# Gate and up projections of the gated layers as 2x2 block products with seven multiplications, down projection in five chunks between them

## The chip, the cores and the metric

The kernel runs on one core of one Trainium2 chip. The metric is device time in microseconds (us), the median of three runs. One execution was profiled; its trace gives the rows below.

## The reference, cut to what matters

Batch 1, 512 tokens, 1024 features, all in float32. A first block (projections, mLSTM, gated MLP, a feed-forward of 4096) is followed by a second block of two layers. Each layer has a gated feed-forward, three attentions and a second gated feed-forward, so there are four gated feed-forwards:

```python
D_FF = 2816

def swiglu(h, w_gate, w_up, w_down):
    return (jax.nn.silu(h @ w_gate) * (h @ w_up)) @ w_down

# in each of the two layers, twice: x = x + 0.5 * swiglu(rmsnorm_2(x, gain), w_gate, w_up, w_down)
```

`rmsnorm_2` scales each token by one number (the reciprocal root of its mean square) and each feature by a gain.

## The kernel before, in words

Activations lie feature-major: a tile is 128 features by 512 tokens, so x is 8 tiles, and the 2816 hidden features are 22 tiles. Every float32 operand of a product is split in a high and a low part (`split`, L201 to L203: ScalarE copies the high part, VectorE subtracts it to get the low one), and each product is three matmuls (`mm3`, L225 to L229: high by high, high by low, low by high). The weights are the stationary operand, 128x128 for one matmul; the activations move, 512 columns at a time. Weights come in units of 128x1024 by DMA on SP's queue (`load_weights`, L209, three raw buffers), and a unit is split in one pass (`split_weights`, L214, three high and three low buffers of 1024).

A gated feed-forward is `ffn` (L870). For each of 22 hidden tiles it takes the gate unit and then the up unit through `gemm_fm` (8 feature tiles by three matmuls of 512 columns each, so 48 matmuls for the pair), into two of three PSUM banks named "g". The operands are `xs`: x times the norm's gain, split, written by the stage ahead of the layer. They lack the norm's factor for each token, `rb`, which is ready only some time into the layer (`norm`, L857, a chain of small steps: sums over features on TensorE, a root on GpSimd, a broadcast on TensorE). So VectorE multiplies both results by `rb` on the way out of PSUM (L885, L887), ScalarE takes the silu, VectorE multiplies the two and the product is split into `hid` (L888, L203). When all 22 tiles are there, the down projection takes each of 8 output tiles through all 22 hidden tiles (66 matmuls in one accumulation, weight units of 8, 8 and 6 tiles), and `residual` (L846) adds half of it to x, writes the next stage's split operands and the square sums. In the last layer the last output tile is done in two halves of 256 tokens, and `g_end` (L918) ends each half: residual, square sums, the final norm, output.

TensorE takes its instructions in the order written, for the first two hidden tiles of a layer (`in_order`, L193). For all else a planner orders the instructions of each engine ahead of time, when the kernel is built. A `Chain` (L104) emits small dependent steps between the products, after a given number of products. The engines then execute their queues in that fixed order. In the first layer the generator behind the norm also multiplies x by the first block's final gain and a second factor `rbx` (L838, eight instructions), and later computes position tables (L950 on).

The lines of `ffn` that the prediction's steps touch:

```python
            self.gemm_fm(og, self.weights(a["w2g"][which, i, 0], KT, P), xs)
            self.gemm_fm(ou, self.weights(a["w2g"][which, i, 1], KT, P), xs)
            while norm.rb is None:
                norm.step()
            ...
            nc.vector.tensor_tensor(t, og, rb, op=ALU.mult)
            nc.scalar.activation(t, t, AF.Silu)
            nc.vector.tensor_tensor(u, ou, rb, op=ALU.mult)
            nc.vector.tensor_tensor(t, t, u, op=ALU.mult)
            self.split(hid[i][0], hid[i][1], t)
```

Of the kernel before, what the change touches and what calls it, by code (L numbers as in the profile page):

```python
# [10 lines left out]
F32 = mybir.dt.float32  # L11
# [20 lines left out]
# columns of the parameter pack  # L32
# [20 lines left out]
# feature-major tiles of the first block's input projection after the first slab  # L53
# [17 lines left out]
# what comes when: the order of the heads and of the projections beside them, the shares of work between two stages of a  # L71
# tile, the products between the steps of a chain, the engines of some elementwise work
# [56 lines left out]
def drain(gen):  # L129
    """run a generator to its end"""  # L130
    while True:
        try:
            next(gen)
        except StopIteration as e:
            return e.value


class Net:
    def __init__(self, ctx, tc, a):
# [11 lines left out]
        self.t, self.chains = 0.0, []  # L151
# [57 lines left out]
    def load_weights(self, src, f):  # L209
        raw = self.wp.tile([P, 1024], F32, name="wraw", tag="wraw", bufs=WBUFS[2])  # L210
        self.last_load = self.nc.sync.dma_start(out=raw[:, :f], in_=src[:, :f])
        return raw

    def split_weights(self, raw, nk, n, pool=False):  # L214
        f = nk * n
        lo = self.wp.tile([P, 1024], F32R, name="wlo", tag="wlo", bufs=WBUFS[0])
        hi = self.wp.tile([P, 1024], F32R, name="whi", tag="whi", bufs=WBUFS[1])
        self.split(hi[:, :f], lo[:, :f], raw[:, :f], pool)
        return (hi[:, :f].rearrange("p (k n) -> p k n", k=nk), lo[:, :f].rearrange("p (k n) -> p k n", k=nk))
# [5 lines left out]
    def mm3(self, out, ah, al, bh, bl, start, stop):  # L225
        mm = self.nc.tensor.matmul
# [1428 lines left out]
```

## Time and profile before

| | |
|---|---|
| median of three runs | 3022.72 us (3022.42 to 3023.36) |
| profiled execution, first to last instruction | 3020.9 us |
| TensorE busy | 2935.9 us, 97%, 13845 matmuls |
| VectorE busy | 1601.3 us, 53% |
| ScalarE busy | 1272.8 us, 42% |
| the four gated layers start at | 873.27, 1571.71, 1942.2 and 2636.4 us |

The profiled execution has no time of its own beside its span; the runs' median is 1.8 us longer than the span. A matmul's duration in the trace holds its way through the array, and the next one starts long before it ends, so the pace of a stream is read from the starts. VectorE's instructions overlap a little in the same way.

### The profile page before, as it was taken

To read this page: it belongs to the slowest core of one execution; us is meant where nothing else is said; L and a number is where in the kernel's file an instruction comes from. 1 tells how busy PE (TensorE), PEld (TensorE's weight loads), DVE (VectorE), ACT (ScalarE), POOL (GpSimd) and SP (SyncE) were. 2 spreads that over 40 slices of the span, in tenths; PEclk is the share of its full clock that TensorE was granted. 3 is DMA by queue.
4 is the path that set the end of the run, shared out by engine and by line. 5 is a ranking of instruction groups with operands and counts; after the bars stand their busy time and mean duration, and the time that the engine had idled before them with its cause. 6 is when DMAs were issued, how large, how long until landed. Compare 5 with 4: busy or idle time off the path is not lost.

```text
span 3020.9 us, 35009 instructions
## 1 busy us (share of the span) xinstructions
PE 2935.9 (97%) x13845; PEld 2387.9 (79%) x13845; DVE 1601.3 (53%) x2388; ACT 1272.8 (42%) x1917; POOL 417.8 (14%) x255
## 2 busy tenths in 40 slices
PE   6999999999999999989999999999999889999998
PEld 5888978888878888876788888888888767888887
DVE  7765665524455443488764443344433887644433
ACT  5665454423333222376743322223223767532322
POOL 4233430000000000243400000000002434100000
PEclk9999999999999999999999999999999999999999
DMA  6334332222223223211022223232322110122222
GB/s 233 111 123 140 137 135 82 92 97 94 95 92 100 92 94 96 89 56 43 29 70 93 96 89 96 94 98 91 96 89 94 57 49 29 63 91 98 92 95 73
DMA packets 79544, 278.06 MB, mean 92 GB/s; under 512 B 8811, under 2 KB 11115, under 8 KB 79380
## 3 DMA queue, kind: packets, MB, share of 16 engines
q1 hardware_dynamic: 79380, 275.82, 28.0%
q8 instruction: 109, 1.79, 0.2%
q14 instruction: 55, 0.45, 0.0%
HBM read 273.69 MB, written 2.10 MB: 91 GB/s over the span
## 4 chain that ended last, share of the span: by engine, by line
PE 89%; DVE 6%; issue 2%; ACT 1%; POOL 1%; DMA 0%; SPq 0%; POOLq 0%; DVEq 0%; ACTq 0%
PE up L227 5%; PE up L229 5%; PE up L228 5%; PE down L228 5%; PE gate L227 5%; PE down L229 5%; PE down L227 5%; PE gate L228 5%; PE gate L229 5%; PE ff L227 4%; PE ff L229 4%; PE ff L228 4%; PE pv L1320 2%; PE ptr L1302 2%; PE wo L229 1%
## 5 line engine op out<-in xcount | busy, mean ns | idle before, releaser
L202 ACT ACTIVATE whi<-wraw 128x1024 fp32r<-128x1024 f32 (+2 forms) x472 | 490.3, 1039 | 1286.9 <-issue 503.1
L203 DVE TENSOR_TENSOR wlo<-wraw,whi 128x1024 fp32r<-128x1024 f32 (+1 forms) x406 | 502.9, 1239 | 428.3 <-ACT whi L202 426.0
L203 POOL TENSOR_TENSOR wlo<-wraw,whi 128x1024 fp32r<-128x1024 f32 (+1 forms) x66 | 155.6, 2361 | 914.8 <-ACT whi L202 903.9
L228 PE MATMUL down<-hid,whi 128*128 128x512 f32 (+1 forms) x726 | 281.6, 388 | 0.0
L229 PE MATMUL down<-hid,wlo 128*128 128x512 f32 (+1 forms) x726 | 281.5, 388 | 0.0
L227 PE MATMUL down<-hid,whi 128*128 128x512 f32 (+1 forms) x726 | 280.9, 387 | 0.0
L887 DVE TENSOR_TENSOR u<-up,rb 128x512 f32<-128x512 f32 x88 | 60.8, 691 | 282.0 <-PE up L229 281.9
L227 PE MATMUL up<-xs,whi 128*128 128x512 f32 x528 | 209.4, 397 | 0.0
L227 PE MATMUL gate<-xs,whi 128*128 128x512 f32 x528 | 208.9, 396 | 0.0
L228 PE MATMUL up<-xs,whi 128*128 128x512 f32 x528 | 208.6, 395 | 0.0
L228 PE MATMUL gate<-xs,whi 128*128 128x512 f32 x528 | 208.5, 395 | 0.0
L229 PE MATMUL up<-xs,wlo 128*128 128x512 f32 x528 | 208.5, 395 | 0.0
L229 PE MATMUL gate<-xs,wlo 128*128 128x512 f32 x528 | 207.8, 394 | 0.0
L272 POOL TENSOR_TENSOR y<-ms,mhalf 128x4 f32<-128x4 f32 (+2 forms) x24 | 27.1, 1128 | 1293.2 <-DVE ms L271 1290.2
L885 DVE TENSOR_TENSOR t<-gate,rb 128x512 f32<-128x512 f32 x88 | 60.8, 691 | 197.5 <-PE gate L229 189.3
L228 PEld LDWEIGHTS down<-hid,whi 128*128 128x128 f32 x726 | 136.4, 188 | 30.7
L227 PEld LDWEIGHTS down<-hid,whi 128*128 128x128 f32 x726 | 136.3, 188 | 30.7
L229 PEld LDWEIGHTS down<-hid,wlo 128*128 128x128 f32 x726 | 136.5, 188 | 29.4
L227 PEld LDWEIGHTS up<-xs,whi 128*128 128x128 f32 x528 | 99.2, 188 | 24.2
L229 PEld LDWEIGHTS up<-xs,wlo 128*128 128x128 f32 x528 | 99.3, 188 | 23.8
L229 PEld LDWEIGHTS gate<-xs,wlo 128*128 128x128 f32 x528 | 99.2, 188 | 23.8
L227 PEld LDWEIGHTS gate<-xs,whi 128*128 128x128 f32 x528 | 99.2, 188 | 23.6
(562 smaller groups left out, 6844.0 us busy)
## 6 DMA issues: line engine op xcount, KB each, us to landing
wraw<-in_w2g SPq DMA_DIRECT2D x176, 512.0 KB, 3.5
wraw<-in_w2d SPq DMA_DIRECT2D x64, 512.0 KB, 3.5
ada<-in_ada SPq DMA_DIRECT2D x48, 512.0 KB, 5.3
wraw<-in_w1f SPq DMA_DIRECT2D x44, 512.0 KB, 3.5
wraw<-in_w1a SPq DMA_DIRECT2D x32, 512.0 KB, 3.4
wraw<-in_w1b SPq DMA_DIRECT2D x32, 512.0 KB, 3.4
wraw<-in_w2f SPq DMA_DIRECT2D x28, 512.0 KB, 3.5
wraw<-in_w2d SPq DMA_DIRECT2D x32, 384.0 KB, 3.0
```

Source lines behind the costliest of these rows:

```text
L202: self.nc.scalar.activation(hi, src, AF.Copy)
L203: (self.nc.gpsimd if pool else self.nc.vector).tensor_tensor(lo, src, hi.bitcast(F32), op=ALU.subtract)
L227: mm(out, ah, bh, start=start, stop=False)
L228: mm(out, ah, bl, start=False, stop=False)
L229: mm(out, al, bh, start=False, stop=stop)
L272: nc.gpsimd.tensor_tensor(y, ms, self.mhalf[:, :n], op=ALU.pow)
L885: nc.vector.tensor_tensor(t, og, rb, op=ALU.mult)
L887: nc.vector.tensor_tensor(u, ou, rb, op=ALU.mult)
L1302: nc.tensor.transpose(tr[:, b * P:(b + 1) * P], p[:, b * P:(b + 1) * P], self.c("ident"))
L1320: nc.tensor.matmul(o, values[b][:, h * P:(h + 1) * P], pt[i][:, b], start=b + i == 0, stop=b + i == NT)
```

## The change

Of the 22 hidden tiles of a gated layer the first three (`PLAIN`) are done as before. For the other 19 the gate and the up tile together are one 2x2 block product: rows gate and up, features 0 to 511 and 512 to 1023, tokens 0 to 255 and 256 to 511. It is computed with 7 products of 4 feature tiles by 256 tokens (84 matmuls of 256 columns) in place of 8 (which would be 48 of 512). The sums of weight blocks are formed for each hidden tile (`g_block_weights`), those of the activations once for each layer (`sums_of`), from x with gain and `rb` in them; all sums are on VectorE. Partial results that several outputs share stay in PSUM while more is added, and are copied out between the products. The last of the seven products of a block is held back until the next block's second product or a down product's third feature tile. The down projection comes in five chunks of hidden tiles, its products standing between the blocks of the next chunk; x is added to after each chunk. Weights for one item are prepared between the products of the item ahead. The high and low parts of a weight unit share one buffer; there are four raw buffers, and 24 big slots in place of 28. In the last layer the last two output tiles of the last chunk end together in two halves of the tokens. TensorE's order is the written one throughout the layer; the other engines stay with the planner.

```diff
-WBUFS = (3, 3, 3)
-SLOTS = 28
+WBUFS = (4, 2, 5, 3)
+SLOTS = 24
+
+CHUNKS = (5, 5, 4, 4, 4)
+
+PLAIN = 3
+H = T // 2
...
     def load_weights(self, src, f):
-        raw = self.wp.tile([P, 1024], F32, name="wraw", tag="wraw", bufs=WBUFS[2])
-        self.last_load = self.nc.sync.dma_start(out=raw[:, :f], in_=src[:, :f])
+        raw = self.wp.tile([P, 1024], F32, name="wraw", tag="wraw", bufs=WBUFS[0])
+        with self.tc.issue_after(self.last_load.ins) if self.last_load else ExitStack():
+            self.last_load = self.nc.sync.dma_start(out=raw[:, :f], in_=src[:, :f])
         return raw
...
+    def kilo(self, name, n):
+        return self.wp.tile([P, 1024 * n], F32R, name=name, tag=f"w{n}k", bufs=WBUFS[1 + n])
...
+    def sums_of(self, up, down, half, pool):
+        v = nc.gpsimd if pool else nc.vector
+        th, tl, b = self.slot("th")[:, :1024], self.slot("tl")[:, :1024], self.slot("bs")[:, :1024]
+        u1, u2, d1, d2 = up[:, :H], up[:, H:], down[:, :H], down[:, H:]
+        ta, tb = self.tmp("ta"), self.tmp("tb")
+        t1, t3, t2, t4 = ta[:, :H], ta[:, H:], tb[:, :H], tb[:, H:]
+        nc.scalar.activation(b[:, :H], u1, AF.Copy)
+        v.tensor_tensor(t1, u2, u1, op=ALU.subtract)
+        v.tensor_tensor(t3, d2, u2, op=ALU.add)
+        nc.scalar.activation(b[:, H:3 * H], down, AF.Copy)
+        v.tensor_tensor(t2, d2, t1, op=ALU.add)
+        v.tensor_tensor(t4, d1, t2, op=ALU.subtract)
+        nc.vector.tensor_tensor(b[:, 3 * H:], u1, b[:, :H].bitcast(F32), op=ALU.subtract)
+        nc.vector.tensor_tensor(half, down, b[:, H:3 * H].bitcast(F32), op=ALU.subtract)
+        for i, t in enumerate((ta, tb)):
+            self.split(th[:, i * T:(i + 1) * T], tl[:, i * T:(i + 1) * T], t, pool)
...
+    def g_block_weights(self, raw):
+        (a21, a22), (a11, a12) = ((r[:, :T], r[:, T:]) for r in raw)
+        s32, s14 = (self.wp.tile([P, 1024], F32, name=name, tag="ws", bufs=WBUFS[1]) for name in ("s32", "s14"))
+        s3, s2, s1, s4 = s32[:, :T], s32[:, T:], s14[:, :T], s14[:, T:]
+        w = {}
+        def part(names, src):
+            n = len(names)
+            t = self.kilo(names[0], n)
+            hi, lo = t[:, :n * T], t[:, n * T:]
+            self.split(hi, lo, src)
...
+        part(["a11"], a11)
+        yield
+        nc.vector.tensor_tensor(s3, a21, a11, op=ALU.subtract)
+        nc.vector.tensor_tensor(s1, a21, a22, op=ALU.subtract)
+        nc.vector.tensor_tensor(s2, a11, s1, op=ALU.subtract)
+        yield
+        part(["s3", "s2"], s32)
+        yield
+        nc.vector.tensor_tensor(s4, a12, s2, op=ALU.subtract)
+        part(["a12"], a12)
+        yield
+        part(["a22"], a22)
+        yield
+        part(["s1", "s4"], s14)
+        yield
...
+    def block(self, w, acts, on, between):
+        def product(out, a, b, first):
+            wh, wl = w[a]
+            n = len(acts)
+            for k in range(n):
+                xh, xl = acts[k][b]
+                self.mm3(out, wh[:, k], wl[:, k], xh, xl, first and k == 0, k == n - 1, skip_group_check=True)
+                self.spend(3 * H * CYCLE)
+            between()
+        e = self.bank("g", "e")[:, :H]
+        product(e, "a11", "b11", True)
+        on("e1", e)
+        g = self.bank("s", "g")[:, :H]
+        product(g, "s3", "t3", True)
+        on("g1", g)
+        self.close_block()
+        product(e, "s2", "t2", False)
+        on("e2", e)
+        f = self.bank("v", "f")[:, :H]
+        product(f, "a12", "b21", True)
+        on("f", f)
+        product(g, "a22", "t4", False)
+        on("g2", g)
+        product(e, "s1", "t1", False)
+        on("e3", e)
+        def last():
+            product(e, "s4", "b22", False)
+            on("e4", e)
...
+        def operands():
+            while norm.rb is None or which == 0 and norm.rbx is None:
+                yield 0.3
+            gains = norm.gain if which == 0 else self.par(("ffn1n0", "ffn2n0", "ffn1n1", "ffn2n1")[which], 0, KT)
+            half = self.halves("xhalf", 4)
+            for k in range(4):
+                t = [self.tmp("xr"), self.tmp("xr")]
+                for i in range(2):
+                    kk = k + 4 * i
+                    nc.vector.scalar_tensor_tensor(t[i], x[:, kk], gains[:, kk:kk + 1], norm.rb, op0=ALU.mult, op1=ALU.mult)
+                    if which == 0:
+                        nc.vector.scalar_tensor_tensor(x[:, kk], x[:, kk], self.par("final1", kk), norm.rbx, op0=ALU.mult, op1=ALU.mult)
+                acts.append(self.sums_of(*t, next(half), False))
+                yield 0.5
+        operands = Chain(self, operands())
...
+        class Up:
...
+            def run(me, w, between):
+                operands.finish()
+                t, u = self.tmp("t"), self.tmp("u")
+                def on(what, o):
+                    if what == "e1":
+                        nc.scalar.activation(t[:, :H], o, AF.Copy)
+                    elif what == "g1":
+                        nc.scalar.activation(u[:, H:], o, AF.Copy)
+                    elif what == "e2":
+                        nc.scalar.activation(u[:, :H], o, AF.Copy)
+                    elif what == "f":
+                        nc.vector.tensor_tensor(t[:, :H], o, t[:, :H], op=ALU.add)
+                        nc.scalar.activation(t[:, :H], t[:, :H], AF.Silu)
+                    elif what == "g2":
+                        nc.vector.tensor_tensor(u[:, :H], o, u[:, :H], op=ALU.add)
+                    elif what == "e3":
+                        nc.vector.tensor_tensor(u[:, H:], o, u[:, H:], op=ALU.add)
+                    else:
+                        nc.scalar.activation(t[:, H:], o, AF.Silu)
+                        nc.vector.tensor_tensor(t, t, u, op=ALU.mult)
+                        keep(me.i, t)
+                self.block(w, acts, on, between)
...
+        class Down:
...
+            def run(me, w, between):
+                o, n = self.bank("g", "down"), me.n
+                act = [hid[me.k0 + k] for k in range(me.nk)]
+                for k, _ in enumerate(self.g_gemm(o, w, act)):
+                    if k == 1:
+                        self.close_block()
+                    between()
+                nc.vector.scalar_tensor_tensor(x[:, n], o, 0.5, x[:, n], op0=ALU.mult, op1=ALU.add)
...
+        class End(Down):
...
+                ends = []
+                for half in range(2):
+                    cols = slice(H * half, H * half + H)
+                    act = [(xh[:, cols], xl[:, cols]) for xh, xl in (hid[me.k0 + k] for k in range(me.nk))]
+                    outs = [self.bank("g", "down")[:, :H] for _ in range(2)]
+                    for o, u in zip(outs, w):
+                        self.gemm_fm(o, u, act)
+                    ends.append(Chain(self, self.g_end(half, cols, outs, acc)))
+                for end in ends:
+                    end.finish()
...
+        items = []
+        for c, nk in enumerate(CHUNKS):
+            downs = [Down(c - 1, n) for n in range(KT)] if c else []
+            for j in range(nk):
+                items.append(ups.pop(0))
+                n = -(-len(downs) // (nk - j))
+                items += downs[:n]
+                downs = downs[n:]
+        items += [Down(last, n) for n in range(KT if gain else KT - 2)] + ([] if gain else [End(last, KT - 2)])
+        for n, item in enumerate(items):
+            if n + 3 < len(items):
+                raws.append(items[n + 3].load())
+            ahead, done = (items[n + 1].prepare(raws[n + 1]) if n + 1 < len(items) else iter(())), []
+            def between():
+                if not done:
+                    try:
+                        next(ahead)
+                    except StopIteration as e:
+                        done.append(e.value)
+            item.run(w, between)
+            while not done:
+                between()
+            w = done[0]
```

## Rows read from the trace of the kernel before

**Rows 1.** The page: busy time of each engine, and the chain by engine.
```profile
PE 2935.9 (97%) x13845; PEld 2387.9 (79%) x13845; DVE 1601.3 (53%) x2388; ACT 1272.8 (42%) x1917; POOL 417.8 (14%) x255
...
PE 89%; DVE 6%; issue 2%; ACT 1%; POOL 1%; DMA 0%; SPq 0%; POOLq 0%; DVEq 0%; ACTq 0%
```
**Rows 2.** Windows: the second gated layer whole, and 19 of its gate/up pairs.
```profile
core 0: us, PE busy (x) PEld busy (x) DVE busy (x) ACT busy (x) POOL busy (x), PEclk, DMA share, GB/s
1571.70:1942.20 370.50, 370.50 (x1599) 299.00 (x1598) 154.80 (x188) 107.59 (x131) 1.02 (x1) 1.00 0.29 93
...
1605.20:1817.00 211.80, 211.80 (x911) 170.81 (x910) 95.71 (x114) 62.13 (x76) 0.00 (x0) 1.00 0.29 94
```
**Rows 3.** Timeline of PE: 512 columns, start of a gate unit and the next.
```profile
902.56 0.40 PE L227 MATMUL gate<-x,whi 128*128 128x512 f32 x1
...
908.14 0.40 PE L227 MATMUL up<-x,whi 128*128 128x512 f32 x1
```
**Rows 4.** Timeline of PE: 256 columns, weights stationary (66 matmuls); then activations stationary.
```profile
2990.36 0.28 PE L227 MATMUL down<-hid,whi 128*128 128x256 f32 x1
...
2998.18 0.28 PE L227 MATMUL down<-hid,whi 128*128 128x256 f32 x1
...
85.45 0.28 PE L227 MATMUL mva<-whi,xn 128*128 128x256 f32 x1
...
86.36 0.28 PE L229 MATMUL mva<-whi,xn 128*128 128x256 f32 x1
```
**Rows 5.** Timeline of DVE: the starts of successive instructions by size and kind.
```profile
1596.82 0.69 DVE L888 TENSOR_TENSOR t<-t,u 128x512 f32<-128x512 f32 x1
1597.43 1.22 DVE L203 TENSOR_TENSOR wlo<-wraw,whi 128x1024 fp32r<-128x1024 f32 x1
1598.57 0.68 DVE L203 TENSOR_TENSOR hid<-t,hid 128x512 fp32r<-128x512 f32 x1
...
3004.71 1.74 DVE L947 TENSOR_TENSOR x<-x,bc_b 128x256 f32<-128x256 f32 x5 [1.26 <-ACT rb L942]
```
**Rows 6.** Groups by line, shapes apart: ScalarE's copies of 1024, 512 and 256 columns.
```profile
L202 ACT ACTIVATE whi<-wraw 128x1024 fp32r<-128x1024 f32 x432 | 457.4, 1059 | 1185.2 <-issue 489.2 <-PE gate L228 265.0 <-PE down L228 178.0
...
L202 ACT ACTIVATE hid<-t 128x512 fp32r<-128x512 f32 x88 | 55.7, 633 | 61.3 <-DVE t L888 61.3
...
L202 ACT ACTIVATE mvh<-mva 128x256 fp32r<-128x256 f32 x8 | 3.0, 376 | 3.3 <-DVE mvl L203 3.3
```
**Rows 7.** Timelines of PE and DVE: start of the second gated layer, its first scaled result.
```profile
1571.71 0.39 PE L227 MATMUL gate<-xs,whi 128*128 128x512 f32 x1
...
1583.90 0.69 DVE L885 TENSOR_TENSOR t<-gate,rb 128x512 f32<-128x512 f32 x1 [2.73 <-ACT rb L308]
```
**Rows 8.** Timelines of PE and DVE: the start of the first gated layer.
```profile
873.27 0.40 PE L227 MATMUL gate<-x,whi 128*128 128x512 f32 x1
...
891.10 0.44 DVE L964 TENSOR_SCALAR posc<-posj 128x4 f32<-128x4 int32 x5
891.46 0.68 DVE L885 TENSOR_TENSOR t<-gate,rb 128x512 f32<-128x512 f32 x1
...
895.50 5.39 DVE L838 SCALAR_TENSOR_TENSOR x<-x,par,rbx 128x512 f32<-128x512 f32 x8 [0.37 <-ACT rbx L308]
```
**Rows 9.** Windows: after a short wait of TensorE; during and after a long one.
```profile
878.70:882.20 3.50, 3.50 (x11) 2.76 (x11) 1.42 (x9) 0.00 (x0) 1.56 (x2) 0.52 0.02 5
...
1291.00:1296.10 5.10, 0.31 (x3) 0.10 (x1) 4.34 (x7) 1.96 (x3) 1.37 (x1) 0.92 0.36 104
1296.10:1301.00 4.90, 4.86 (x20) 4.45 (x21) 3.05 (x11) 4.63 (x11) 0.00 (x0) 0.50 0.00 0
```
**Rows 10.** Timeline of DVE: the end, second half of the tokens.
```profile
3008.06 0.42 DVE L922 SCALAR_TENSOR_TENSOR x<-down,x 128x256 f32<-128x256 f32 x1 [1.60 <-PE down L229]
...
3014.49 1.74 DVE L947 TENSOR_TENSOR x<-x,bc_b 128x256 f32<-128x256 f32 x5 [1.26 <-ACT rb L942]
```
**Rows 11.** The page: the weight loads of gate and up, median time to landing.
```profile
wraw<-in_w2g SPq DMA_DIRECT2D x176, 512.0 KB, 3.5
```

More of the change, by code (lines that the diff above doesn't have):

```diff
@@ L841, in block1_rest @@
         box = Chain(self, gen())
-        box.rb = None
+        box.rb = box.rbx = None
+        box.gain = fgn
         return nx, box
@@ L890, in ffn @@
-        nx = self.act_slots("xs", KT) if gain else None
-        acc = self.acc("acc")
-        units = (8, 8, 6)
-        for n in range(KT if gain else KT - 1):
-            o = self.bank("g", "down")
-            k0 = 0
-            for i, nk in enumerate(units):
-                self.gemm_fm(o, self.weights(a["w2d"][which, n, i], nk, P), hid, k0, i == 0, i == 2)
-                k0 += nk
-            self.residual(n, o, 0.5, nx, gain, acc)
-            if not gain:
-                nc.scalar.activation(self.x[:, n], self.x[:, n], AF.Copy, scale=self.par("final2", n))
@@ L902, in ffn @@
-        if gain:
-            return nx, self.norm(acc, keep="rkeep")
-        ws = [self.weights(a["w2d"][which, KT - 1, i], nk, P) for i, nk in enumerate(units)]
-        order.enter_context(self.in_order("end"))
-        for half in range(2):
-            o, cols = self.bank("g", "down")[:, :256], slice(256 * half, 256 * half + 256)
-            act = [(xh[:, cols], xl[:, cols]) for xh, xl in hid]
-            k0 = 0
-            for i, nk in enumerate(units):
-                self.gemm_fm(o, ws[i], act, k0, i == 0, i == 2)
-                k0 += nk
-            end = Chain(self, self.g_end(half, cols, o, acc))
@@ new lines, in ffn, with keep, __init__, load @@
+        operands = Chain(self, operands())
+        hid = {}
+        def keep(i, h):
+            hid[i] = self.act_slots("hid", 1)[0]
+            self.split(hid[i][0], hid[i][1], h)
+        class Plain:
+            def __init__(me, i):
+                me.i = i
+            def load(me):
+                return [self.load_weights(a["w2g"][which, me.i, u], 1024) for u in range(2)]
+            def prepare(me, raw):
+                out = []
+                for r in raw:
+                    out.append(self.split_weights(r, KT, P))
+                    yield
+                return out
+            def run(me, w, between):
+                og, ou = self.bank("g", "gate"), self.bank("g", "up")
+                for n, (o, u) in enumerate(((og, w[1]), (ou, w[0]))):
+                    for k, _ in enumerate(self.g_gemm(o, u, xs)):
+                        if k % 3 == 2:
+                            between()
+                while norm.rb is None:
+                    norm.step()
+                t, u = self.tmp("t"), self.tmp("u")
+                nc.vector.tensor_tensor(t, og, norm.rb, op=ALU.mult)
+                nc.scalar.activation(t, t, AF.Silu)
+                nc.vector.tensor_tensor(u, ou, norm.rb, op=ALU.mult)
+                nc.vector.tensor_tensor(t, t, u, op=ALU.mult)
+                keep(me.i, t)
@@ new lines, in ffn, with load, prepare, run @@
+        class End(Down):
+            def load(me):
+                return [Down.load(Down(me.c, n)) for n in (KT - 2, KT - 1)]
+            def prepare(me, raw):
+                out = []
+                for r in raw:
+                    out.append(self.split_weights(r, me.nk, P))
+                    yield
+                return out
+            def run(me, w, between):
+                ends = []
[8 more added lines that the diff above has]
+                    end.finish()
```

122 lines of the change are left out of this document (80 added, 42 removed).

## The prediction

> **What bounds the kernel now.** I read the page first: TensorE is busy 97% of the span, and the chain that ended last is 89% TensorE and 6% VectorE [rows 1]. Then the windows of one gated layer: in 370.5 us TensorE is busy for all of them, VectorE for 155 and ScalarE for 108 [rows 2]. So inside these layers nothing but matmul time counts, and VectorE has some 215 us of room in each. Last the starts in the timeline, since durations overlap: a unit of 24 matmuls of 512 columns takes 908.14 - 902.56 = 5.58 us, 0.2325 each, so a gate/up pair takes 11.16 us [rows 3].
>
> **The blocks.** 19 pairs in each of four layers, 76 in all, become 84 matmuls of 256 columns. The same operands in the same roles run at 256 columns in the last tile of the kernel before: 66 matmuls from 2990.36 to 2998.18, 0.1185 each [rows 4]. A block is then 84 x 0.1185 = 9.95 us, a gain of 1.21, and 76 give 92 us. Where activations are stationary eight matmuls took 0.91 us, 0.114 each [rows 4]: that would give 9.56 us a block and 122 us in all. I take 0.1185, the row with the same roles, and keep 122 as the far end. Seven eighths of the columns thus don't give seven eighths of the time.
>
> A rule of the Trainium skill speaks against such a change. "TensorE: Matmul & The Clock Gate", section Part 3, says that a weight load overlaps a running matmul only where the two use different row groups, and its section on LDWEIGHTS puts a load at the number of weight columns over 1.2 GHz, here 107 ns. Full loads that don't overlap would make each matmul 0.1185 + 0.107 us as an estimate, a block 18.9 us, and the kernel some 590 us slower. The row does not agree: those 66 matmuls each had their own load and still started every 0.1185 us [rows 4].
>
> **What VectorE gets for it.** Its paces by start to start: 512 columns 0.61 us, 1024 columns 1.14 us [rows 5]; 256 columns 1.74 / 5 = 0.35 [rows 5]; a scalar_tensor_tensor of 512 columns 5.39 / 8 = 0.67 [rows 8]. A block's weights are four sums and three low parts of 512 columns and two low parts of 1024: 7 x 0.61 + 2 x 1.14 = 6.55. Its results are three sums of 256 and two steps of 512: 2.27. So 8.8 us a block, where a pair took 2 x 1.14 + 4 x 0.61 = 4.7. A chunk's down product needs a split of 640 or 512 columns (about 0.74, between the two paces, or 0.61) and one addition to x (0.61): 1.22 to 1.35. A block and two downs of four tiles take VectorE 8.8 + 2.4 = 11.2 us and TensorE 9.95 + 2 x 12 x 0.2325 = 15.5: 72%. ScalarE has five copies of weights (3 x 0.63 + 2 x 1.06 = 4.0) and some 2.5 of results [rows 6]. On average all of it lies beside matmuls.
>
> **Where it does not: the start of each layer.** The block operands need `rb` in them, so they can't be made ahead. For each of four pairs of feature tiles: two scalings, five instructions of 256 and three of 512 columns, 2 x 0.67 + 5 x 0.35 + 3 x 0.61 = 4.9 us, 19.7 for a layer. `rb` comes 12.2 us into the layer (1583.90 - 1571.71) [rows 7]. Then VectorE owes, before the first block can start, 19.7 for operands, 2 x 2.4 for the results of two plain tiles (they free PSUM banks), 1.1 for the last plain split, 0.6 for the first weight block and about 1 of hand-overs with ScalarE: 12.2 + 27.2 = 39.4 us. Three plain tiles end at 3 x 11.16 plus 0.9 for the norm's small matmuls = 34.4: a stall of 5.0. The second product wants three sums, a copy on ScalarE and a low part (1.8 + 1.06 + 1.14 = 4.0) where the first covers 12 x 0.1185 = 1.42: 2.6 more, 8 in all. In the first layer the wait is for `rbx` too: VectorE starts at 895.50, 22.2 us in, and scales x as well (5.4): 22.2 + 25.1 + 2.4 + 0.6 + 1 = 51.3, where the third plain tile ends 11.16 after 902.56, at 40.5 [rows 3, 8]; with the 2.6 a stall of 13. Sum 3 x 8 + 13 = 37. Were the operands taken ahead of the third plain tile's gate split, that tile would wait: 12.2 + 19.7 + 2.4 + 1.1 = 35.4 against 23, 12 a layer, about 60 in all. If waits of this kind hide well it is some 15.
>
> After a wait TensorE is slow for a while: behind the 4.83 us wait the granted clock was 0.50 in 4.9 us, and after a short one 0.52 in 3.5 us, which is the 1.2 GHz level [rows 9]. That loses 1.7 to 2.4 us; I take 2 a layer, 8 (0 to 12).
>
> **The other 64 blocks.** A partial result must be copied before its bank is added to: the first copy has one product, 1.42 us, as cover. Behind it can stand a 1024-column copy on ScalarE, 1.06 + 0.38 [rows 6], which with the hand-over is 0.1 to 0.3 late. With VectorE now and then late too I take 0.25 a block, 16 us (0 to 1 each, 0 to 64).
>
> **Small terms.** Loads: a block's two wait until the block ahead has read its raw tiles, since four buffers hold two blocks; they land in 3.5 us each [rows 11], and 15 us of products hide them. The SP queue carries nothing else there; if that cover went, the block's weights would be late by the same amount. The layer's end: eight downs of 2.79 us each, with split, addition, next operands and squares on VectorE (0.61 + 0.61 + 0.67 + 0.61 = 2.5): no lag to speak of, 1 us at each of three hand-overs, 3 (0 to 8). The kernel's end: the chain from 3008.06 to the output now has two tiles a half (about 1 us more), and the first half's chain, once hidden beside 66 matmuls, has 24 x 0.1185 = 2.8 us of cover and stands in front of the second's on TensorE, 2 more [rows 10]: 3 (1 to 6). Fewer slots and the shared split buffers elsewhere: no row shows such a wait, 0 (-2 to 10).
>
> **The sum**, against the span of 3020.9: -92 + 37 + 8 + 16 + 3 + 3 = -25, so 2996, and with the 1.8 us that the median lies above the span, **2998 us**.
>
> **Rivals.** (a) Nearly all hides: starts 18, clock 4, ends 6, blocks nothing: -64, **2959**; with the faster pace 2929. For it: a fifth of VectorE's time is free even in a full cycle, and the planner does take later work early: the tables' L964 ran at 891.10, ahead of the eight scalings written before it [rows 8]. Against: 27 us of operands and results behind one late factor.
> (b) VectorE sets the pace of every block, which makes it slower. If it takes a block's weights only after the first down's result, then from that point TensorE has one down (2.8 to 3.5) and the first product (1.42) as cover, while VectorE and ScalarE need the addition 0.6, the block's first part 0.6, and the 4.0 above, with the last result of the block before (1.2) in the way: 6.4 against 4.2 to 4.9, about 2 us a block. 64 x 2 in place of 16 is +87: **3110**. It decides from (92 - 37 - 8 - 6) / 64 = 0.64 us a block. For it: fixed queues, planned with times that need not be the chip's. Against: the L964 row.
> (c) Small waits between products hold the clock down. At 1.7 us a block [rows 9], 76 blocks lose 129: **3127**. The Trainium skill has this in "TensorE: Matmul & The Clock Gate", section "A second HAM failure mode", where cycling through PSUM banks made TensorE idle between groups and the clock went to and fro. By that rule the blocks would do the same; the trace shows it only behind waits as above.
> That the change does not do what it says I leave out: the seven products stand in the code.
>
> **How the numbers follow.** The forecast has 0.45 (its own range 2975 to 3025), (a) 0.22, (b) 0.25, (c) 0.04, and 0.04 for slots or loads that cost tens of us. A tenth lies below 2948 and a tenth above 3075. A measurement of this kernel tells 0.2%, 6 us. Of the forecast's 0.45, 0.37 is faster, 0.04 the same, 0.04 slower; with (a) that is faster 0.59, same 0.05, slower 0.36.
>
> **What would show it.** Rows of 256 columns for e, g and f, some 6400, 0.118 us apart; VectorE busy near 2140 us by durations; waits of TensorE of 5 to 13 us at the third plain tile or the first block of each layer and clock 0.5 behind them; small waits elsewhere. It is wrong if blocks of the middle chunks take over 10.6 us each, or if the starts cost over 60.

## The result

The changed kernel takes 3039.2 us (3032.7 to 3044.6, four runs) beside 3022.9 for the kernel before: ratio 1.0054, 95% interval 1.0038 to 1.0070, half a per cent slower. The profiled execution has a span of 3032.6 us, 11.7 above the one of before; the medians are 16.3 apart. All stretches below are read from each kernel's profiled execution.

Of the page after, the busy time and the chain by engine, which answer to [rows 1]:

```profile
PE 2865.6 (94%) x16539; PEld 2470.9 (81%) x16539; DVE 2057.9 (68%) x3350; ACT 1514.4 (50%) x2579; POOL 417.2 (14%) x255
...
PE 64%; DVE 13%; issue 4%; DMA 3%; ACT 3%; POOL 1%; POOLq 0%; SPq 0%; DVEq 0%; ACTq 0%
...
wraw<-in_w2g SPq DMA_DIRECT2D x176, 512.0 KB, 4.3
```

TensorE is busy 70 us less, and the time is longer: the gain was made, and more than that is idle. VectorE's share of the chain doubled. The loads land in 4.3 us where they took 3.5 [rows 11]; no wait of TensorE names one, though 3% of the chain that ended last now runs through them.

The same stages in three profiled executions, from the starts of the matmuls in the timelines (us; a mix stage holds the three attentions between two gated layers; the last column is the best version, found below):

| stage | before | after | change | best |
|---|---|---|---|---|
| first block, to the first gate product | 873.3 | 883.6 | +10.3 | 876.5 |
| gated layer 1 | 375.5 | 378.3 | +2.8 | 363.6 |
| mix stage 1 | 322.9 | 329.2 | +6.3 | 319.7 |
| gated layers 2 and 3 | 740.8 | 729.9 | -10.9 | 701.6 |
| mix stage 2 | 323.9 | 330.4 | +6.5 | 322.1 |
| gated layer 4 | 371.7 | 365.7 | -6.0 | 351.2 |
| from the last down product on | 12.8 | 15.5 | +2.7 | 15.5 |

So the layers, which the change is about, are 14 us shorter, and 26 us were lost where its own products don't run.

**The blocks run as forecast.** PE's timeline in a middle block (start, duration, line, output and operands):

```profile
1700.40 0.29 PE L240 MATMUL e<-th,s 128*128 128x256 f32 x1
1700.53 0.28 PE L238 MATMUL f<-bs,a 128*128 128x256 f32 x1
1700.64 0.29 PE L239 MATMUL f<-xhalf,a 128*128 128x256 f32 x1
1700.77 0.28 PE L240 MATMUL f<-bs,a 128*128 128x256 f32 x1
```

0.12 apart, also across the change of the bank. Added up over its 84 starts a block takes 9.95 us in the median of 76, 10.02 in the mean; three are over 10.6 (10.9 to 11.5), all in the first layer.

**The wait.** PE's waits over the whole execution (what was waited for, total, times, longest):

```profile
PE up L238 <- DVE t L1043: 56.6, 4, 14.6
PE ptr L1562 <- DVE p L1607: 11.3, 12, 1.6
```

Four waits, one a layer, 57 us in the first line. PE's and then VectorE's timeline at the second layer, which starts at 1591.12:

```profile
1609.45 0.40 PE L240 MATMUL gate<-xs,wsp 128*128 128x512 f32 x1
1624.33 0.79 PE L238 MATMUL up<-xs,wsp 128*128 128x512 f32 x1 [14.48 <-DVE t L1043]
1624.92 0.63 PE L239 MATMUL up<-xs,wsp 128*128 128x512 f32 x1
1625.35 0.63 PE L240 MATMUL up<-xs,wsp 128*128 128x512 f32 x1
```
```profile
1603.62 0.69 DVE L935 TENSOR_TENSOR s<-wraw 128x512 f32<-128x512 f32 x1 [2.95 <-DMA wraw<-in_w2g]
1604.23 1.41 DVE L1006 SCALAR_TENSOR_TENSOR xr<-x,par,rb 128x512 f32<-128x512 f32 x2
1605.55 0.69 DVE L936 TENSOR_TENSOR s<-wraw 128x512 f32<-128x512 f32 x1
...
1623.27 0.41 DVE L898 TENSOR_TENSOR tb<-xr,ta 128x256 f32<-128x256 f32 x1
1623.60 0.68 DVE L1043 TENSOR_TENSOR t<-gate,rb 128x512 f32<-128x512 f32 x1
```

The up product of the second plain tile needs a fourth PSUM bank of three, so it waits until VectorE has read the first plain tile's gate result (L1043). `rb` is there at about 1603.6, and VectorE then takes 20 us of operands (L1006, L895 to L901) and of the first block's weights (L935 to L941) ahead of that one instruction of 0.68 us. It never pauses: no wait of VectorE's own explains it, only its order. Layers 3 and 4 wait in the same place (14.6 and 14.5 us). In the first layer VectorE reads the first plain tile's results early, and the wait, 13.1 us, stands at the third plain tile's up product, which needs the bank of the second one's gate. There the order also puts a step of 0.28 us (L308), which the norm's second factor `rbx` needs, behind other work, and TensorE waits for it. PE's timeline, before and after:

```profile
894.20 0.63 PE L301 MATMUL bc_b<-ft,sel 40*128 40x128 f32 x4 [0.79 <-DVE ft L297]
```
```profile
908.26 1.08 PE L312 MATMUL bc_b<-ft,sel 40*128 40x128 f32 x4 [4.30 <-DVE ft L308]
```

### The profile page after: what moved, and what is told of

Read it like the earlier page. It is cut to its first block, busy times and chain, and to the rows that moved or that the text cites. A ratio compares the mean times of both kernels' runs of the same rounds, so it can differ in the third digit from the quotient of the medians.

```text
span 3032.6 us, 42186 instructions
## 1 busy us (share of the span) xinstructions
PE 2865.6 (94%) x16539; PEld 2470.9 (81%) x16539; DVE 2057.9 (68%) x3350; ACT 1514.4 (50%) x2579; POOL 417.2 (14%) x255
## 4 chain that ended last, share of the span: by engine, by line
PE 64%; DVE 13%; issue 4%; DMA 3%; ACT 3%; POOL 1%; POOLq 0%; SPq 0%; DVEq 0%; ACTq 0%
PE down L238 5%; PE down L240 5%; PE down L239 5%; PE e L238 4%; PE e L240 4%; PE ff L238 4%; PE ff L240 4%; PE ff L239 4%; PE e L239 4%; DMA wraw<-in_w2g 3%; PE g L240 2%; PE g L239 2%; PE g L238 2%; PE pv L1580 2%; PE ptr L1562 1%
## 5 line engine op out<-in xcount | busy, mean ns | idle before, releaser
L209 ACT ACTIVATE wsp<-wraw 128x1024 fp32r<-128x1024 f32 (+2 forms) x384 | 340.9, 888 | 362.8 <-issue 124.5
L210 DVE TENSOR_TENSOR wsp<-wraw,wsp 128x1024 fp32r<-128x1024 f32 (+2 forms) x318 | 320.5, 1008 | 187.3 <-ACT wsp L209 186.7
L210 POOL TENSOR_TENSOR wsp<-wraw,wsp 128x1024 fp32r<-128x1024 f32 (+1 forms) x66 | 156.3, 2371 | 946.1 <-ACT wsp L209 912.1
L240 PE MATMUL down<-hid,wsp 128*128 128x512 f32 (+1 forms) x712 | 279.3, 392 | 0.0
L238 PE MATMUL down<-hid,wsp 128*128 128x512 f32 (+1 forms) x712 | 279.1, 392 | 0.0
L239 PE MATMUL down<-hid,wsp 128*128 128x512 f32 (+1 forms) x712 | 278.7, 391 | 0.0
L210 DVE TENSOR_TENSOR s<-s,s 128x1024 fp32r<-128x1024 f32 x152 | 183.6, 1218 | 5.0 <-ACT s L209 5.0
L238 PE MATMUL e<-th,s 128*128 128x256 f32 x608 | 170.9, 281 | 1.3 <-ACT t L1065 1.3
L240 PE MATMUL e<-th,s 128*128 128x256 f32 x608 | 171.5, 282 | 0.0
L239 PE MATMUL e<-tl,s 128*128 128x256 f32 x608 | 170.3, 280 | 0.0
L209 ACT ACTIVATE s<-s 128x1024 fp32r<-128x1024 f32 x152 | 157.6, 1050 | 20.7 <-PE up L240 15.0
L240 PEld LDWEIGHTS down<-hid,wsp 128*128 128x128 f32 x712 | 133.8, 188 | 30.9
L239 PEld LDWEIGHTS down<-hid,wsp 128*128 128x128 f32 x712 | 133.8, 188 | 25.2
L238 PEld LDWEIGHTS down<-hid,wsp 128*128 128x128 f32 x712 | 133.9, 188 | 24.6
L238 PEld LDWEIGHTS e<-th,s 128*128 128x128 f32 x608 | 114.7, 189 | 1.5 <-ACT t L1065 1.5
L240 PEld LDWEIGHTS e<-th,s 128*128 128x128 f32 x608 | 114.4, 188 | 0.0
```

The source lines that it names most:

```text
L209: self.nc.scalar.activation(hi, src, AF.Copy)
L210: (self.nc.gpsimd if pool else self.nc.vector).tensor_tensor(lo, src, hi.bitcast(F32), op=ALU.subtract)
L238: mm(out, ah, bh, start=start, stop=False)
L239: mm(out, ah, bl, start=False, stop=False)
L240: mm(out, al, bh, start=False, stop=stop)
```

## The experiments

Two theories at first. Order: the planner puts the wrong instruction last. Amount: VectorE owes so much behind `rb` that the wait only moves.

**1. Results first.** Operands and the first block's weights are queued on VectorE behind the plain tiles' results.

```diff
+BEHIND = (1, 1, 2, 2)
+                while len(freed) < BEHIND[k]:
+                    yield 0.3
+                with self.tc.issue_after(freed[BEHIND[k] - 1].ins):
                     (scalings and sums_of of pair k)
...
-                nc.vector.tensor_tensor(u, ou, norm.rb, op=ALU.mult)
+                freed.append(nc.vector.tensor_tensor(u, ou, norm.rb, op=ALU.mult))
...
+                while me.i == PLAIN:
+                    with self.tc.issue_after(freed[PLAIN - 2].ins):
                         (next step of g_block_weights)
```

> The changed kernel with one thing more: at the start of each gated layer the operands of the blocks and the sums and splits of the first block's weights are queued on VectorE behind the results of the plain tiles (operands 1 and 2 behind the first plain tile's up product, operands 3 and 4 and the first block's weights behind the second's). No work is added or taken away. Theory 1 (order): the 14.7 us wait at the second plain tile's up product exists because VectorE takes some 20 us of operands and weights ahead of the instruction that frees its PSUM bank; with the results first it falls below 1 us, and what stays is the 5 to 10 us in front of the first block. Four layers gain 5 to 9 us each: 3003 to 3020 us, from 3039. Theory 2 (amount): VectorE owes the same work before the first block in any order, so the wait only moves there, 13 to 16 us in each layer, and the time stays within 6 us of 3039.

3028.1 us, ratio to the kernel before 1.0022 (1.0011 to 1.0032): 11 us less, where the first theory wanted 19 to 36 and the second at most 6. PE's waits in the first products of the second layer:

```profile
PE e L240 <- DVE bs L901: 5.6, 2, 4.3
PE g L240 <- DVE tl L211: 1.9, 1, 1.9
PE e L239 <- ACT th L210: 1.2, 1, 1.2
PE e L240 <- DVE tl L211: 1.1, 1, 1.1
```

The wait at the plain tile is gone (2.0 us stay in the first layer), and some 10 us stand in the first block, for operands and their low parts. A layer's time over the pace is the time from its first gate product to its last down product, less 0.2325 us for each matmul of 512 columns, 0.1185 for each of 256 and some 2 us for the norm's small ones. In the last layer it falls only from 17.9 to 15.7 us: 9.2 us are waits, and most of the rest is the clock, since from 2699.10 to 2712.00 us, between these waits, the granted clock is 0.50, the 1.2 GHz level. So it is the amount, in the main: in this order too VectorE is late by about 10 us. The 11 us of the medians are not all in the layers: the profiled execution, the slowest of its eight runs (3038.0 us), has the four layers 6.7 us shorter than the changed kernel and the mix stages longer.

**2 and 3. Four plain tiles,** with results first (`PLAIN = 4`, `BEHIND = (1, 1, 2, 3)`) and without.

> As the kernel before it in this call, with four plain tiles in each layer in place of three (operands 3 and 4 behind the second and the third plain tile, the first block's weights behind the third). A plain tile more costs TensorE 11.16 - 9.95 = 1.21 us a layer and puts 11.16 us of matmuls in front of the first block. If only the start of the layers was mis-sized, all of its waits go: below 2 us a layer in place of 14.7 (18 to 21 in the first), and 4 x 1.2 us come on top: 3039 - 60 + 5 = 2984, 2980 to 2992. If other waits were hidden behind them (the first blocks' weights late, ScalarE late), 2 to 5 us a layer stay: 2993 to 3005.

> The changed kernel with four plain tiles in place of three, and the order on VectorE left to the planner. Theory 1 (order): the wait stands at the second plain tile's up product, far ahead of the first block, so another plain tile behind it changes nothing of it: 13 to 15 us a layer stay and the time is 3039 + 5 = 3044 (3036 to 3050). Theory 2 (amount): 11.16 us more of matmuls beside the same work of VectorE: the wait shrinks by about 10 us a layer, 3039 - 40 + 5 = 3004 (2998 to 3012).

With results first 2997.2 us, ratio 0.9916 (0.9901 to 0.9930); alone 3023.5, ratio 1.0004 (0.9995 to 1.0014). Alone, the wait stays at its place but is 10.6 to 10.7 us in layers 2 to 4 in place of 14.5 (15.3 in the first, from 13.1): between the two theories, and neither expectation of the time holds. Together 5.2 us over the pace are left in the last layer, from 17.9, which is the second case that was expected, with other waits behind the first. The two are worth 11 and 16 us by themselves and 42 together, by the medians; in the profiled executions the four layers are 6.7, 10.9 and 39.8 us shorter. The order brings the wait to where more matmuls can cover it, and the additional tile is that cover. Of the second layer's waits, in the first block, two are left:

```profile
PE e L240 <- DVE tl L211: 1.8, 1, 1.8
PE g L241 <- DVE s L211: 1.6, 1, 1.6
```

**4. The kernel before with 24 slots.**

```diff
-SLOTS = 28
+SLOTS = 24
```

> The kernel before with 24 slots in place of 28 and nothing else. The changed kernel is 10.3 us later than the kernel before when the first gated layer starts, where none of its own code has run. If the four slots are the cause, this kernel starts its first gated layer at 882 to 885 us in place of 873.3, with a wait of about 4 us of the output projection for its operands near 460 us, and takes 3030 to 3036. If the order of the loads or the shared split buffers are, the layer starts within 2 us of 873.3 and the time is within 4 us of 3022.8.

3028.8 us, ratio 1.0017 (1.0008 to 1.0026): neither expectation holds, and the slots alone cost half. The layer starts at 878.5 us in place of 873.3, but the wait at the output projection was not among it (0.6 us there), so another cause holds that one.

**5. The hand-over to the mix stage.** VectorE's timeline at the end of the first layer, in the changed kernel, and GpSimd's beside it:

```profile
1258.30 2.39 DVE L214 SCALAR_TENSOR_TENSOR xs<-x,par,xs 128x512 fp32r<-128x512 f32 x1 [0.47 <-ACT xs L213]
1260.61 2.89 DVE L336 TENSOR_TENSOR acc<-acc,sq 128x512 f32<-128x512 f32 x1
...
1264.89 0.75 DVE L214 SCALAR_TENSOR_TENSOR xs<-x,par,xs 128x512 fp32r<-128x512 f32 x1 [0.79 <-ACT xs L213]
1265.56 0.68 DVE L336 TENSOR_TENSOR acc<-acc,sq 128x512 f32<-128x512 f32 x1
```
```profile
1257.73 2.41 POOL L210 TENSOR_TENSOR wsp<-wraw,wsp 128x1024 fp32r<-128x1024 f32 x1 [365.28 <-ACT wsp L209]
1260.50 2.45 POOL L210 TENSOR_TENSOR wsp<-wraw,wsp 128x1024 fp32r<-128x1024 f32 x1 [0.36 <-ACT wsp L209]
```

The same two lines take 0.75 and 0.68 us alone and 2.39 and 2.89 beside a GpSimd split, and each ends 0.55 us behind that split's end (1260.69 and 1260.14, 1263.50 and 1262.95). GpSimd holds VectorE up. The Trainium skill has this in "SBUF — State Buffer", section "Who interferes with whom": a VectorE instruction with two inputs in SBUF contends with a GpSimd instruction that reads SBUF, the port pair that they share is an exclusive lock, and the order of issue decides which of the two waits. These rows agree: both splits start ahead of the VectorE instruction, by 0.57 and 0.11 us, and VectorE waits. On the results-first kernel with four plain tiles:

```diff
-  self.weights(a["w2f"][l, FM2_AT[key]], KT, P, pool=True)
+  self.weights(a["w2f"][l, FM2_AT[key]], KT, P, pool=key != "dq0")
-  [self.weights(src[i], 4, 256, True) for i in range(2)]
+  [self.weights(src[i], 4, 256, name != "vd") for i in range(2)]
```

> The kernel with results first and four plain tiles (2997.2 us), and the splits of the first three weight units of the mix stage (both of vd, and dq0) on VectorE in place of GpSimd. Theory (shared time): at the end of a gated layer VectorE is short of time for the last residuals, and its instructions that stand beside a GpSimd split take 2.4 to 2.9 us in place of 0.7; without the three GpSimd splits none does, the small sums come about 6 to 7 us into the mix stage in place of 10.2 and 10.6, TensorE gets its full clock back earlier, and each of two mix stages is 3 to 7 us shorter: 2983 to 2991. Rival (backlog): five steps of VectorE for each down of 2.79 us are the cause, three more of 1.14 us make it worse: mix stages 1 to 3 us longer, 2999 to 3004.

2986.2 us, ratio 0.9875 (0.9859 to 0.9892), 11 us less, as the theory said. The norm's small sums stand 5.9 us behind the last down product (before 6.0, changed 10.6), and the mix stages take 325.6 and 325.4 us from that product in place of 332.6 and 333.0. VectorE now has the splits to do, and is earlier:

```profile
1253.46 1.22 DVE L211 TENSOR_TENSOR wsp<-wraw,wsp 128x1024 fp32r<-128x1024 f32 x1
1254.60 0.74 DVE L215 SCALAR_TENSOR_TENSOR xs<-x,par,xs 128x512 fp32r<-128x512 f32 x1
1255.26 0.69 DVE L337 TENSOR_TENSOR acc<-acc,sq 128x512 f32<-128x512 f32 x1
```

**6. A long last chunk in its place,** `CHUNKS = (4, 4, 4, 4, 6)`, on the same base of 2997.2 us.

> The kernel with results first and four plain tiles (2997.2 us), with chunks of 4, 4, 4, 4 and 6 tiles in place of 5, 5, 4, 4 and 4: the eight last down products take 4.2 us in place of 2.8, so VectorE has 1.4 us more for each. Theory (shared time): only the GpSimd splits hold VectorE up, and they last 2.4 us as before; with the longer products the backlog is smaller, the small sums come 7 to 9 us into the mix stage, gain 2 to 3 us a stage; but a down product less stands between the blocks, where VectorE then has less cover: 2993 to 3000. Rival (backlog): the mix stages start as in the kernel of before, gain 4.5 us each in three layers: 2982 to 2988.

3017.0 us, ratio 0.9976 (0.9966 to 0.9987). The hand-over is cured as well: the small sums come at 6.2 us, as the rival said, where the theory had 7 to 9. The collision is still there (VectorE's instructions beside the splits take 2.37, 2.20 and 2.17 us), but a product of 4.2 us leaves time for it. So the loss needed both, the GpSimd splits and products as short as 2.8 us. But the four layers are 28.5 us longer in sum in the profiled executions, which neither foresaw: over the pace of their matmuls the blocks have 46 us in place of 25 and the down products 13 in place of 4, in the first block of each layer (16 to 23 us, from 14 to 20) and in single later ones, in waits up to 2 us for VectorE's last results. The down products between the blocks are VectorE's cover, and this division of them is the worse one.

**7 to 9. The first block.** The loads and buffers of the change put into the kernel before; the split buffer alone put into it; and the four gmlp constants moved out of the slots into buffers that only the blocks use, on the kernel of experiment 5.

```diff
-  lo = self.wp.tile([P, 1024], F32R, name="wlo", tag="wlo", bufs=WBUFS[0])
-  hi = self.wp.tile([P, 1024], F32R, name="whi", tag="whi", bufs=WBUFS[1])
+  both = self.wp.tile([P, 2048], F32R, name="wsp", tag="wsp", bufs=WBUFS[0])
+  hi, lo = both[:, :1024], both[:, 1024:]
```
```diff
-  lng, lnb = self.slot("lng", F32)[:, :1024], self.slot("lnb", F32)[:, :1024]
+  spare = lambda n: self.wp.tile([P, 1024], F32, name=n, tag="w1k", bufs=WBUFS[2])
+  lng, lnb = spare("lng"), spare("lnb")
```

> The kernel before, with 28 slots, and of the change only the handling of weights: loads held to the order written, four buffers for raw weights in place of three, one buffer for the high and low part of a unit, and the smaller memory for DMA descriptors. If these are the other half of the 10.3 us in the first block, its first gated layer starts at 876 to 879 us in place of 873.3 and the time is 3026 to 3030. If the slots are all of it and the rest is the planner's other choices, it starts within 1.5 us of 873.3 and the time is within 3 us of 3022.8.

> The kernel before, 28 slots, three raw buffers and its own order of loads, with one buffer of 8 KB for the high and low part of a weight unit in place of two of 4 KB (and the smaller memory for DMA descriptors, which makes room). Theory (shared split buffers): the high part, once read for the last time, no longer comes free by itself, ScalarE and VectorE get another order in the first block, the output projection waits about 4.5 us for its operands near 470 us, the first gated layer starts at 879 to 883 us and the time is 3028 to 3033. Rival (loads): the fourth raw buffer and the order of loads did it; here the layer starts within 2 us of 873.3 and the time is within 3 us of 3023.

> As the kernel before it in this call, and the four constant tiles of the first block's gmlp stand in buffers of the blocks' weights, which lie idle there, so that the 24 slots serve the rest. If the four missing slots are what makes the first block late, the first gated layer starts at 876 to 880 us in place of 886, and the time falls by 5 to 8 us against that kernel. If the order of loads or the shared split buffers are, it moves by less than 2 us.

3032.1 us, ratio 1.0032 (1.0018 to 1.0045); 3025.7, ratio 1.0008 (0.9998 to 1.0017); and 2984.9, ratio 0.9876 (0.9861 to 0.9891), no gain on experiment 5. The first gated layer starts at 881.0, 883.7 and 885.5 us. So 7 is later than either of its cases; 8 has the late start of its theory, 0.7 us beyond its range, and the time of its rival; 9 has the time of its second case, which would have cleared the slots. The times are mixed; the stretches are not. From the first matmul of `gvb` to that of `wo`, from there to the first gate product, and the first small transpose of the start:

| kernel | slots serve | split buffers | gvb to wo | wo to gate | start |
|---|---|---|---|---|---|
| before | 28 | own | 144.0 | 411.8 | 19.2 |
| before, 24 slots (4) | 24 | own | 148.0 | 411.8 | 19.9 |
| before, loads and split buffer (7) | 28 | shared | 144.3 | 418.1 | 19.7 |
| before, split buffer (8) | 28 | shared | 144.4 | 418.5 | 19.8 |
| changed | 24 | shared | 149.3 | 417.7 | 19.7 |
| hand-over splits (5) | 24 | shared | 147.8 | 416.0 | 20.2 |
| constants moved (9) | 28 | shared | 145.1 | 417.3 | 24.4 |
| the same, own buffers (10) | 28 | own | 145.2 | 411.1 | 24.1 |

Four missing slots cost 3 to 5 us in the gmlp part (the first block's gated MLP), wherever they are missing. A shared buffer costs 4 to 7 behind it, wherever it is shared. The loads' order and the fourth raw buffer are neither cause: 7 and 8 differ by 0.4 us at most in both stretches. Nor is the smaller memory for DMA descriptors, which the changed kernel and all made from it have too: 10 has it, and 411.1. PE's wait in the second stretch, in the kernel before with the shared buffer:

```profile
PE wo L227 <- ACT mg L202: 4.5, 1, 4.5
```

Moving the constants gave 2.7 us back and lost 4.2 at the start, so the first layer of experiment 9 starts 4.4 us later than that of 5; its four layers are 4.6 us shorter, for a reason that no run tells, and the total showed nothing. In experiment 8 the mix stages were some 3 to 5 us shorter than before, which hid most of the loss (experiment 12 comes back to them), and 3.3 us of the late start stand ahead of `gvb`, unexplained.

**10. Own buffers again,** on experiment 9, for the high and low part of a weight unit and of a block's two pairs of weight sums, and **11. five plain tiles** on that (`PLAIN = 5`).

> The kernel with results first, four plain tiles, hand-over splits on VectorE and gmlp constants outside the slots (2984.9 us), and the high and low part of a weight unit in buffers of their own again, as in the kernel before. Theory (shared split buffers, with the slots): the first gated layer starts at 872 to 877 us in place of 885.5, without the 4 us wait of the output projection, and the mix stages shorten by 0 to 2 us: 2973 to 2979. Rival (chance of the order): it starts at 881 to 886 again and the time stays within 3 us of 2985.

> As the kernel before it in this call, with five plain tiles in each layer. Theory (amount): with four, 4.5 to 7 us of a layer still go to waits and half clock in its first blocks, since VectorE works without a pause from the norm's factor on; another 11.16 us of matmuls takes them away for 1.21 us: 3 to 4.5 us a layer, 12 to 18 us less than that kernel. Rival: what is left is no backlog but the chain inside a block's first products (sum, copy, low part), which another plain tile does not shorten: 1 us a layer more, 4 to 6 us above it.

2975.0 us, ratio 0.9836 (0.9819 to 0.9852): the time as the theory said, in part by luck. The wait of the output projection is gone (0.7 us from 4.0), but the first layer starts at 880.6 and not at 872 to 877, for the late start; that is 4.9 us, and 6.6 more came in the four layers, where none were expected. Then 2966.9, ratio 0.9813 (0.9799 to 0.9828): 8 us less, where 12 to 18 were expected. The waits at the layers' starts are gone but for 2.6 us in the first (layers 2 and 3 are 0.2 us over the pace in sum, from 10.5), so it was the amount: the four layers gave the 13.2 us expected. But each mix stage is 2.8 us longer, with nothing changed in it.

**12. The constants' loads later.** SP's queue at the start in experiment 11 (start, issue time, line, target and source):

```profile
5.73 0.34 SPq L698 DMA_DIRECT2D lng<-in_lnt  x1
6.11 0.44 SPq L698 DMA_DIRECT2D lnb<-in_lnt  x1
6.60 0.45 SPq L700 DMA_DIRECT2D ws<-in_wsb  x1
7.75 0.33 SPq L700 DMA_DIRECT2D bsb<-in_wsb  x1
9.53 2.25 SPq L434 DMA_DIRECT2D ada<-in_ada  x2
```

Their new buffers are free from the first moment, so 2 MB for a stage 300 us later go ahead of the first loads of the modulation.

```diff
+        with self.tc.issue_after(self.last_load.ins):
             (the four dma_starts of lng, lnb, ws, bsb)
```

> The kernel with five plain tiles and own buffers (2966.9 us), and the loads of the four gmlp constants queued behind the weight loads of the first block's projections in place of ahead of the first loads of the modulation. In every kernel that has these constants outside the slots the first small transpose of the start runs at 24.1 to 24.4 us, in all others at 19.2 to 20.7. If the 2 MB of constants ahead of the modulation's loads are the cause, it runs at 19 to 21 us, the first gated layer starts at 875 to 878 us in place of 881.5, and the time is 2960 to 2964. If the start is late by chance or for the buffers themselves, it runs at 24 us again and the time stays within 2 us of 2966.9.

```profile
6.25 0.82 SPq L434 DMA_DIRECT2D ada<-in_ada  x2
```

2952.9 us (2948.2 to 2954.8, five runs), ratio 0.9766 (0.9753 to 0.9779): 2.3% faster than the kernel before, 2.8% below the changed one. The transpose runs at 19.9 us and the first layer starts at 876.5, as expected. But 14 us came where 5 were expected: the mix stages took 319.7 and 322.1 us where experiment 11 had some 328 in each, with the same matmuls in the same order on TensorE. The windows of the first mix stage, whole and for 14 us of it, show TensorE's clock as the difference (experiment 11, then 12; length, busy time of PE, PEld, DVE, ACT, POOL, granted clock, DMA share, GB/s):

```profile
1245.73:1573.86 328.13, 308.59 (x1619) 248.67 (x1618) 242.01 (x457) 214.65 (x410) 111.33 (x66) 0.95 0.16 52
1426.73:1440.73 14.00, 13.87 (x39) 9.12 (x38) 6.20 (x19) 6.41 (x13) 4.21 (x3) 0.51 0.01 1
```
```profile
1239.88:1559.76 319.88, 298.81 (x1620) 241.89 (x1619) 242.42 (x457) 214.57 (x410) 111.43 (x66) 0.98 0.16 53
1420.88:1434.88 14.00, 11.59 (x58) 7.97 (x57) 11.55 (x21) 10.03 (x19) 3.69 (x2) 1.00 0.06 19
```

In the 14 us that begin 181 us behind the last down product TensorE has 39 matmuls at 0.51, the 1.2 GHz level, and 58 at 1.00. The other kernels with early small sums follow: 319 to 320 us at 0.98 (experiment 8), 323 and 324 at 0.97 (before), 325 to 326 at 0.96 or 0.97 (5 and 10). What sets such a stretch off in one kernel and not in another stays open.

## Why the prediction was wrong

The sign was wrong. The time lies outside the forecast's own range (2975 to 3025) and inside the wide one (2948 to 3075), by chance: the wide one made room for slow blocks, and the blocks were not slow. (A tenth above 3075 also does not fit the 0.25 given to a rival at 3110.) It had -25 us against the profiled span, and +11.7 came: 17 of the 37 between lie in the layers, 10 in the mix stages, 10 in the first block.

- **The blocks, -92: right.** 84 times 0.1185 is 9.95, the median measured. The Trainium skill's rule on weight loads ("TensorE: Matmul & The Clock Gate", section Part 3: a load overlaps a running matmul only where the row groups differ), weighed against [rows 4], does not hold in 76 blocks either. The same section excepts loads into a background weight buffer, which the prediction left out; no run here shows where a load goes. In the best version layers 2 to 4 show nearly the whole gain: 17 blocks at 1.21 are 20.6, and its layers 2 and 3 take 350.8 each where 370.4 stood. The first layer gained 11.9.
- **The layers' starts, 37 and 8 for the clock: the step that failed.** It let VectorE take the plain tiles' results ahead of the operands. The planner did not, and the plain tiles lie some 70 us further over their pace than before, where 45 were forecast for the starts and 60 named as a sign of being wrong: 57 in the four waits, most of the rest in the clock behind them and the wait for `rbx`. The 57 us are near the "about 60 in all" that the prediction priced for that case and left out of its sum, but in three layers at the second plain tile, 20 us of other work ahead of one short instruction. The row that showed the planner taking later work early (L964 in [rows 8]) was used for a rival and not against this step. Experiment 1 shows a second error: with the assumed order 9.2 us of waits remain in the last layer, where 8 were forecast, and with the clock its blocks lie 15 us over their pace, where 10 were: VectorE takes the first block's other weights in between, and of these only 0.6 us were counted ahead of the first block.
- **The clock:** behind the 14.5 us wait six matmuls start 0.43 apart in place of 0.23, and the product takes 7.0 us for 5.6: 1.4 us a layer, 2 forecast. The shorter waits of experiment 1 cost more by the clock, some 6 us in the last layer.
- **The other 64 blocks, 16: too high.** All 76 lie 5 us over the pace in sum, and 4 of these in the first layer. With that rival (b) falls: from 0.64 us a block it would have decided. Rival (c) falls by the clock, here behind the wait and in the middle of the second layer (windows: length, busy time of PE, PEld, DVE, ACT, POOL, granted clock, DMA share, GB/s):

```profile
1624.30:1631.40 7.10, 7.07 (x25) 5.68 (x26) 7.10 (x14) 4.61 (x7) 0.00 (x0) 0.79 0.00 0
1660.00:1800.00 140.00, 139.59 (x977) 129.99 (x976) 100.36 (x155) 62.81 (x112) 0.00 (x0) 1.00 0.32 104
```

Between the blocks TensorE is busy for 139.6 of 140 us at a granted clock of 1.00, and VectorE for 100.

- **The hand-overs, 3: too low by 10.** VectorE's sum of 2.5 us a down product was right by its own paces; that GpSimd splits the next stage's weights just there was not counted. The trace of before has the same collision once at that place, with no queue behind it:

```profile
1250.36 2.36 DVE L207 SCALAR_TENSOR_TENSOR xs<-x,par,xs 128x512 fp32r<-128x512 f32 x1 [0.79 <-ACT xs L206]
```

- **Slots and split buffers, 0 (-2 to 10): wrong.** The 10.3 us of the first block are the two causes of the table, 5.3 and 5.9 us less 0.9 elsewhere, in a stage whose own code did not change. "No row shows such a wait" was true of the kernel before, which had the buffers.
- **The end, 3: right** (2.7).

Rival (a), that nearly all hides at 2959, is what the best version does (2952.9), with an order, a cover, buffers and splits that the change did not have.

## What to carry to other kernels

Where an engine falls behind a late factor, ask which instruction frees a PSUM bank and put it first by hand, then give TensorE matmuls that need none of the factor: order and cover were worth 42 us together, and 11 and 16 alone. When a change takes memory or merges buffers, price the stages that it doesn't touch, and measure them by stretches between fixed products, since two effects of 5 us can cancel in the total; read the granted clock with each stretch, since unchanged stages moved by 3 to 8 us with it. Before work is spread over VectorE and GpSimd, look for VectorE instructions that take 2 to 3 us at a size that takes 0.7.

## What was not expected of the hardware

A GpSimd split of 1024 columns (2.4 us) can lengthen a VectorE instruction of 512 columns beside it from 0.7 to 2.4 or 2.9 us; the same three splits on VectorE itself (1.22 us each) made each mix stage 7 us shorter. And four loads of 0.5 MB, issued ahead of others, put these off by 3.3 us at the queue (9.53 against 6.25) and the first transpose by 4.2 (24.1 against 19.9).
